# A Strassen-type feed-forward layer: forming the combined input blocks in feature-major layout from copies of transposed blocks

## The chip, the cores and the metric

The kernel runs on one core of one Trainium2 chip. The metric is the device time of one execution in microseconds (us). Before the change three runs took 2793.43, 2794.3 and 2796.57 us; the median is 2794.3 us.

The core has five engines that run side by side, each through its own queue, in order: PE (matrix products, and transposes as products with an identity matrix), DVE (the vector engine), ACT (the scalar engine), POOL (GpSimd) and SP (which issues DMAs here). PE writes only to PSUM, a small memory of eight banks, each of 512 float32 values in each of 128 partitions. SBUF is the large working memory.

## The reference

Two pre-norm layers work on a sequence of 1024 tokens of width 1024. Each has a mixer (attention), a feed-forward part (`conv_ffn`) and an embedding gate. What the change touches lies between the mixer and the feed-forward part:

```
x = x + y                                       # y: the mixer's output
x = x + conv_ffn(rms_norm(x, ffn_norm[i]), w_ffn_up[i], ...)

def conv_ffn(h, w_up, conv_w, conv_b, w_down):
    u = h @ w_up                                # 1024 -> 2 x 2816
    up = pad(u, one token on either side)
    u = up[:, :-2] * conv_w[0] + up[:, 1:-1] * conv_w[1] + up[:, 2:] * conv_w[2] + conv_b
    gate, val = split(u, 2)
    return (silu(gate) * val) @ w_down
```

## The kernel before

**Precision.** Every large product is float32 in three passes: each operand is split into a high part (a copy to the format fp32r, by ACT) and a low part (the operand less its high part, by DVE), and PE adds high x high, high x low and low x high (`mm3`, L172 to L177).

**The up-projection.** `ffn` (L309) multiplies the normed input h with `w_up` by a scheme of seven products in place of eight (Strassen's, in Winograd's form). h is cut into four quarters, by halves of the features and of the tokens. Besides the quarters themselves it needs four combinations of them, numbered 1 to 4; combination 1 overwrites a quarter that lies in `self.H`, the others go to `self.T`. For the weights the same kind of sums is made on POOL (`sums`, L395), and each weight operand is split by ACT and DVE (`prepare`, L413, with `parts`, L321). The first column of 128 features (`plain`, L335) is computed without the scheme, with the four quarters, and gives time to form the combinations. From f = 1 on each column takes six or seven products of 12 matmuls (`product`, L430), in the order `UP1` for the first and `UP` for the others.

**From the mixer to h.** The mixer ends in `gemm_part` (L242), the output projection, whose second half of the columns is walked in eight blocks of 128 tokens. For each block t, when its residual add on DVE is done (L258), `fold_mixed` (L1522) runs: the block's sum of squares on ACT (L222) and its reciprocal root on POOL (L182, L183), the scaling of block t-1 on DVE (L226), and `ready` for block t-2. `ready` (L1506) calls `to_hT` (L229). This transposes the block on PE, four 128x128 tiles into one PSUM bank, twice (L236); ACT copies the bank to the high part (L238), DVE subtracts for the low part (L239). Blocks 6 and 7 follow as `rest` during `plain`'s first half: block 6 after three steps of the gate column, block 7 after three of the value column.

**The combinations.** `ready` also keeps the scaled block, token-major (one token to a partition). With block q of the last four, `mixes(q)` (L265) forms the four combinations of blocks q-4 and q in that layout: three differences on POOL (L271, L272, L274) and one on DVE (L273), each 128x512. Later, `turn_mix` (L277) brings one combination of one block pair to feature-major layout: four transposes on PE into a PSUM bank (L283), then for combination 1 one ACT copy and one DVE subtraction of 128x512 (L288, L289), for the others two of each of 128x256 (L296, L297). Its sixteen calls a layer stand in the program order in `plain`'s second half (combinations 2 and 3, one after every second step) and in f = 1 (combinations 1 and 4, L646 to L648).

**What sets the order.** The program's order is written by hand, and every engine takes its instructions in that order. The framework adds the semaphore waits between engines. Small PSUM tiles (`tb`) rotate through four one-bank buffers: an output projection's block uses one and `to_hT` two, a turn one, and a column's first products two. SBUF tiles of 4 KB per partition come from a pool of 37 (`u`).

**The functions between.** `conv` (L360) is the convolution of a column: one ACT pass with weight and bias (L363), two DVE passes (L364, L366), and SiLU on ACT for the gate (L369). `evict` (L449) moves and adds products between PSUM banks.

Of the kernel before, what the change touches and what calls it, by code (L numbers as in the profile page):

```python
# [11 lines left out]
F32 = mybir.dt.float32  # L12
# [13 lines left out]
P = 128  # L26
S = 1024
# [79 lines left out]
class Kern:  # L107
# [118 lines left out]
        self.nc.vector.scalar_tensor_tensor(xs, x, r, gb, op0=ALU.mult, op1=ALU.mult)  # L226
        return xs

    def to_hT(self, src, t):  # L229

        nc = self.nc
        for h in range(2):
            ps = self.tb()
            v = ps.rearrange("p (k c) -> p k c", k=4)
            for k in range(4):
                nc.tensor.transpose(v[:, k, :], src(4 * h + k), self.ident)  # L236
            oh, ol = self.hT2(slice(4 * h, 4 * h + 4), slice(t * P, (t + 1) * P))
            nc.scalar.copy(oh, v)  # L238
            nc.vector.tensor_sub(ol, v, oh.bitcast(F32))  # L239


    def gemm_part(self, W, k0, load, after):  # L242
# [34 lines left out]
    def turn_mix(self, n, j):  # L277

        nc = self.nc
        src = self.tm[j].pop(n)  # L280
        ps = self.tb()
        for k in range(4):
            nc.tensor.transpose(ps[:, k * P:(k + 1) * P], src[:, k * P:(k + 1) * P], self.ident)  # L283
        jk = slice(j * P, (j + 1) * P)
        if n == 1:
            v = ps.rearrange("p (k c) -> p k c", k=4)
            h, l = self.hT2(slice(0, 4), slice(512 + j * P, 512 + (j + 1) * P))
            nc.scalar.copy(h, v)  # L288
            nc.vector.tensor_sub(l, v, h.bitcast(F32))  # L289
            return  # L290
        if n not in self.T:
            self.T[n] = [[self.u([P, 2, 512], F32R, "T") for _ in range(2)] for _ in range(2)]
        for q in range(2):
            v = ps[:, q * 256:q * 256 + 256].rearrange("p (k c) -> p k c", k=2)
            h, l = (self.T[n][x][q][:, :, jk] for x in range(2))
            nc.scalar.copy(h, v)  # L296
            nc.vector.tensor_sub(l, v, h.bitcast(F32))  # L297
# [1179 lines left out]
    def build(self):  # L1477
        nc, a = self.nc, self.a
        srcs = []
        for u in range(6):  # L1480
            srcs += [(a["w_in"][u, q], 768) for q in range(4)]
        srcs += [(a["w_out"][h, 2 * k + q], 1024) for k in range(2) for h in range(2) for q in range(2)]
        srcs += self.ffn_srcs(a, 0)
        ends = [len(srcs)]
        srcs += [(a["w_gate"][0, h, q], 1024) for h in range(2) for q in range(4)]
        for p in range(8):
            srcs += [(a["w_inc"][q, p], 1024, 0.125 if q == 0 else None) for q in range(3)]
        srcs += [(a["w_outc"][h, 2 * k + q], 1024) for k in range(2) for h in range(2) for q in range(2)]
        srcs += self.ffn_srcs(a, 1)
        ends.append(len(srcs))  # L1490
        srcs += [(a["w_gate"][1, h, q], 1024) for h in range(2) for q in range(4)]
        W = Weights(self, srcs, ends)
        self.setup(W)

        stats, scaled = {}, {}
        self.keep, self.tm = {}, {}

        def stage1(t):
            stats[t] = self.norm_stats(t)

        def stage2(t):
            for q in sorted(stats):
                if q <= t:
                    scaled[q] = self.norm_scale(*stats.pop(q))

        def ready(t, mixed=False):  # L1506
            stage2(t)
            for q in sorted(scaled):
                if q <= t:
                    x = scaled.pop(q)  # L1510
                    self.to_hT(lambda k: x[:, k * P:(k + 1) * P], q)
                    if mixed:
                        self.keep[q] = x
                        if q >= 4:
                            self.mixes(q)

        def fold(t, mixed=False):
            stage1(t)
            stage2(t - 1)
            ready(t - 2, mixed)  # L1520

        def fold_mixed(t):  # L1522
            fold(t, True)

        def rest(mixed=False):
            stage2(NT - 1)
            ready(NT - 2, mixed)
            yield
            ready(NT - 1, mixed)
            yield  # L1530

        def rest_ple(row):
            for t in range(4, NT):
                fold(t)
                yield
            self.load_gain(row)
            yield from rest()

        seen = set()

        def ready0(t):
            for q in range(t, min(t + 3, NT)):
                if q not in seen:
                    seen.add(q)
                    stage1(q)
                    self.X[q] = None
            stage2(t + 1)
            ready(t)

        W.nraw = 0  # L1550
        stage1(0)
        stage2(0)
        W.pump(1)
        ready(0)
        W.pump(1)
        stage1(1)
        W.pump(2)
        W.nraw = 2
        seen.update((0, 1))
        def load0(t):  # L1560
            if t == 0:
                self.load_gain(a["ffn_norm"][0:1, :])
            self.load_x(t, a["x"][t * P:(t + 1) * P, :])

        def load1(t):
            if t == 0:
                self.load_gain(a["ffn_norm"][1:2, :])
            self.load_x(t, self.x_dram[t])

        self.even(W, ready0, load0, fold_mixed)  # L1570
        for i in range(2):
            nc.sync.dma_start(self.cw[:, i], a["convp"][i])
        if self.stop == "mix0":
            return self.dump()
        for i in range(2):
            self.ffn(i, W, rest(True), lambda: self.ple_pre(i), fold)
            if self.stop == f"ffn{i}":
                return self.dump()
            if i == 0:
                def after(h, t):  # L1580
                    if h:
                        fold(t)
                        nc.sync.dma_start(self.x_dram[t], self.X[t])
                self.ple(0, W, rest_ple(a["attn_norm"][1:2, :]), after)
                if self.stop == "ple0":
                    return self.dump()
                self.odd(W, rest(), load1, fold_mixed)
                if self.stop == "mix1":
                    return self.dump()
            else:  # L1590
                def finish(t):
                    stage2(t)
                    for q in sorted(scaled):
                        nc.sync.dma_start(self.out[q * P:(q + 1) * P, :], scaled.pop(q))

                def after1(h, t):
                    if h:
                        stage1(t)
                        finish(t - 1)
                self.ple(1, W, rest_ple(a["final_norm"][None, :]), after1)  # L1600
                finish(NT)
# [95 lines left out]
```

## Time and profile before

| | |
|---|---|
| median of three runs | 2794.3 us |
| the profiled execution | 2795.31 us |
| its span, first to last instruction | 2793.3 us |
| transposes of the combinations on PE (L283) | 128, 18.8 us |
| transposes of the blocks on PE (L236) | 384 in all, 51.6 us |
| differences of blocks on POOL (L271, L272, L274) | 8 each, 10.3, 12.7 and 13.5 us |
| differences of blocks on DVE (L273) | 8, 8.4 us |
| layer 0: first and last transposes of combinations | 724.7 and 764.4 us |
| layer 1: the same | 2028.8 and 2068.8 us |

How to read the lines. A line of the timeline gives the start in us, the duration in us, the engine, the line of the program, the operation, the output and its inputs by the program's names, sizes and a count; several like instructions in a row are merged, and the duration is then that of all. In square brackets is the time for which the engine was idle just before, and what ended the wait. A line of the groups gives the count, then the busy time in us and the mean of one in ns, then the idle time before them. A line of the waits gives who waited for whom, the total in us, how many times, and the longest. A line of the list of one source line's instructions gives shortest, median and longest duration in ns. A line of the stretches gives the stretch, its length, the busy time of PE, of its weight loads, of DVE, ACT and POOL with the number of instructions, the granted clock of PE, and the DMAs.

### The profile page before, as it was taken

Reading aid. Unit: us, or ns where it says so; the run is one execution under the profiler, and the core shown is the slowest. Engines: PE = TensorE matmul, PEld = TensorE weight load, DVE = VectorE, ACT = ScalarE, POOL = GpSimd, SP = SyncE. Lnnn points to the kernel's source line nnn. Section 1 sums busy time; section 2 is a strip of 40 time slices with the busy share of each in tenths; the row PEclk is TensorE's granted clock in tenths of the full one; section 3 lists DMA queues with packets and bytes.
Section 4 is the critical chain, followed back from the end, with each engine's and each line's share of the span. In section 5 each row is a group of like instructions: output and inputs, shape, how many; then the busy total and the mean of one; then the engine's idle time right before and its main releaser. Section 6 shows DMA issues by size and latency. Waiting matters only on the chain. (4 is left out here: it accounts for less than half of the span.)

```text
span 2793.3 us, 37183 instructions
## 1 busy us (share of the span) xinstructions
PE 2734.1 (98%) x13776; PEld 2265.0 (81%) x13776; DVE 1920.2 (69%) x3004; ACT 1405.2 (50%) x2727; POOL 668.1 (24%) x756
## 2 busy tenths in 40 slices
PE   8999999999999999999999999999999999999998
PEld 8988877777788888888887878877878888888887
DVE  5677878775777777677635666666677777767753
ACT  4455567563444444534523666766344444453532
POOL 2222751000544444100101001000244444400000
PEclk9999999999999999999999999999999999999999
DMA  4000001101134333833211111124023343472411
GB/s 161 1 24 24 27 9 46 46 16 33 39 144 150 133 118 148 297 110 128 87 68 71 37 59 48 38 70 161 16 89 136 130 151 136 170 275 83 147 46 61
DMA packets 101700, 260.77 MB, mean 93 GB/s; under 512 B 12048, under 2 KB 18320, under 8 KB 101520
## 3 DMA queue, kind: packets, MB, share of 16 engines
q1 hardware_dynamic: 101520, 258.40, 26.1%
q8 instruction: 109, 1.79, 0.3%
q14 instruction: 71, 0.58, 0.1%
HBM read 200.16 MB, written 58.20 MB: 92 GB/s over the span
## 5 line engine op out<-in xcount | busy, mean ns | idle before, releaser
L446 PE MATMUL b<-H,op 128*128 128x512 f32 x2016 | 482.5, 391 | 9.9 <-DVE T L297 6.9
L446 PEld LDWEIGHTS b<-H,op 128*128 128x128 f32 x2016 | 379.2, 189 | 90.1 <-issue 7.5
L446 PE MATMUL S<-T,op 128*128 128x512 f32 x1512 | 364.1, 390 | 2.9 <-ACT m L464 2.7
L175 PE MATMUL b<-hi,H 128*128 128x512 f32 (+1 forms) x896 | 337.9, 377 | 1.5 <-ACT H L1297 1.5
L446 PEld LDWEIGHTS S<-T,op 128*128 128x128 f32 x1512 | 283.2, 188 | 63.3 <-ACT m L464 3.2
L176 PE MATMUL b<-lo,H 128*128 128x512 f32 (+1 forms) x896 | 329.8, 368 | 0.8 <-DVE lo L165 0.8
L177 PE MATMUL b<-hi,H 128*128 128x512 f32 (+1 forms) x896 | 330.2, 368 | 0.3 <-DVE H L1298 0.3
L182 POOL TENSOR_SCALAR col<-col 128x1 f32<-128x1 f32 (+2 forms) x100 | 29.4, 294 | 1253.3 <-ACT xs L222 1074.1
L582 PE MATMUL S<-do,do 128*128 128x512 f32 x924 | 276.7, 390 | 3.6 <-ACT do L323 2.2
L582 PE MATMUL b<-do,do 128*128 128x512 f32 x924 | 275.5, 389 | 0.0
L582 PEld LDWEIGHTS S<-do,do 128*128 128x128 f32 x924 | 172.5, 188 | 41.9 <-ACT do L323 3.0
L582 PEld LDWEIGHTS b<-do,do 128*128 128x128 f32 x924 | 173.4, 188 | 36.2
L986 ACT ACTIVATE P<-S,col 128x1024 f32<-128x1024 f32 x128 | 143.4, 1121 | 111.5 <-DVE col L977 109.0
L324 DVE TENSOR_TENSOR op<-sm,op 128x512 fp32r<-128x512 f32 x168 | 131.2, 781 | 87.8 <-ACT op L323 87.0
L175 PEld LDWEIGHTS b<-hi,H 128*128 128x128 f32 x896 | 169.4, 189 | 23.0 <-ACT H L1297 1.9
L177 PEld LDWEIGHTS b<-hi,H 128*128 128x128 f32 x896 | 169.1, 189 | 21.7 <-DVE H L1298 1.2
L176 PEld LDWEIGHTS b<-lo,H 128*128 128x128 f32 x896 | 169.6, 189 | 20.8 <-DVE lo L165 2.3
L324 DVE TENSOR_TENSOR op<-raw,op 128x512 fp32r<-128x512 f32 x126 | 161.1, 1298 | 3.8 <-ACT op L323 3.4
L977 DVE TENSOR_REDUCE col<-S 128x1 f32<-128x1024 f32 x128 | 153.1, 1217 | 10.8 <-PE S L974 9.9
L175 PE MATMUL b<-H,hi 128*128 128x512 f32 x384 | 157.3, 410 | 0.2 <-ACT H L238 0.2
L177 PE MATMUL b<-H,lo 128*128 128x512 f32 x384 | 150.1, 391 | 0.0
L176 PE MATMUL b<-H,hi 128*128 128x512 f32 x384 | 149.8, 390 | 0.2 <-DVE H L239 0.2
(199 smaller groups left out, 5275.2 us busy)
## 6 DMA issues: line engine op xcount, KB each, us to landing
raw<-in_w_up SPq DMA_DIRECT2D x88, 512.0 KB, 4.4
we<-in_w_down SPq DMA_DIRECT2D x44, 512.0 KB, 5.1
g_dram<-cv SPq DMA_DIRECT2D x44, 512.0 KB, 2.6
wt_dram<-we SPq DMA_DIRECT2D x88, 256.0 KB, 3.1
wd<-wt_dram SPq DMA_DIRECT2D x88, 256.0 KB, 2.9
wd<-in_w_down SPq DMA_DIRECT2D x66, 256.0 KB, 5.3
G<-g_dram SPq DMA_DIRECT2D x64, 256.0 KB, 5.4
raw<-in_w_inc SPq DMA_DIRECT2D x24, 512.0 KB, 3.8
```

Of the source, the lines that this page charges most:

```text
L175: mm(out, st[0], mv[0], start=start, stop=False)
L176: mm(out, st[0], mv[1], start=False, stop=False)
L177: mm(out, st[1], mv[0], start=False, stop=stop)
L182: self.nc.gpsimd.tensor_scalar(r, ss, inv_n, EPS, op0=ALU.mult, op1=ALU.add)
L324: nc.vector.tensor_sub(o[:, 1], src, o[:, 0].bitcast(F32))
L446: mm(out, w[:, x, k], moving(n, y, k), start=(fresh and k + x + y == 0), stop=(k == 3 and x == 1), skip_group_check=True)
L582: mm(out[t], A[:, x, t * P:(t + 1) * P], B[:, y], start=(fresh and k == 0 and x + y == 0), stop=(k == NC - 1 and x == 1), skip_group_check ...
L977: nc.vector.tensor_reduce(nm, ps, axis=AX.X, op=ALU.max, negate=True)
L986: nc.scalar.activation(p, ps, AF.Exp, bias=nm, accum_out=e["s"][:, c:c + 1])
```

## The change

`to_hT` gets a tile `keep` when the block belongs to the inputs of the feed-forward part. After the high copy and the low subtraction of each half, ACT copies the same PSUM bank a second time, in full precision, into that tile. `mixes` is as it was, but works on these feature-major copies, and not on the scaled token-major block. `turn_mix` no longer transposes: it takes the combination from SBUF, where the ACT copies and the DVE subtractions before took it from PSUM. Their number and sizes stay, as do their places in the program order.

```diff
-    def to_hT(self, src, t):
+    def to_hT(self, src, t, keep=None):
...
             nc.scalar.copy(oh, v)
             nc.vector.tensor_sub(ol, v, oh.bitcast(F32))
+            if keep is not None:
+                nc.scalar.copy(keep[:, h * 512:h * 512 + 512], ps)
...
         src = self.tm[j].pop(n)
-        ps = self.tb()
-        for k in range(4):
-            nc.tensor.transpose(ps[:, k * P:(k + 1) * P], src[:, k * P:(k + 1) * P], self.ident)
         jk = slice(j * P, (j + 1) * P)
         if n == 1:
-            v = ps.rearrange("p (k c) -> p k c", k=4)
+            v = src.rearrange("p (k c) -> p k c", k=4)
...
         for q in range(2):
-            v = ps[:, q * 256:q * 256 + 256].rearrange("p (k c) -> p k c", k=2)
+            v = src[:, q * 256:q * 256 + 256].rearrange("p (k c) -> p k c", k=2)
...
                     x = scaled.pop(q)
-                    self.to_hT(lambda k: x[:, k * P:(k + 1) * P], q)
                     if mixed:
-                        self.keep[q] = x
-                        if q >= 4:
-                            self.mixes(q)
+                        self.keep[q] = self.u([P, S], F32, "keep")
+                    self.to_hT(lambda k: x[:, k * P:(k + 1) * P], q, self.keep.get(q))
+                    if mixed and q >= 4:
+                        self.mixes(q)
```

## The prediction

> **What bounds the kernel now.** I read the page first, then the whole-span waits of the matrix engine, then the timeline of every engine from the last mixer product to the second feed-forward column, in both layers.
>
> ```profile
> span 2793.3 us, 37183 instructions
> PE 2734.1 (98%) x13776; PEld 2265.0 (81%) x13776; DVE 1920.2 (69%) x3004; ACT 1405.2 (50%) x2727; POOL 668.1 (24%) x756
> PE b L446 <- DVE T L297: 6.9, 2, 3.4
> PE b L446 <- DVE op L324: 3.0, 2, 1.5
> L283 PE MATMUL b<-ident,tm 128*128 128x128 f32 x128 | 18.8, 275 | 0.0
> ```
>
> PE is busy 98% of the span, so work taken off PE shortens the kernel where PE is really the last to be ready. The transposes that go are the 128 of L283. But two of PE's few waits, once per layer each, are for VectorE (DVE) in this very stretch, so there the vector side sets the pace. The profiled run took 2795.31 us, 2.0 more than its span; the median of the three runs is 2794.3, so I add differences to 2794.3. What a measurement of this kernel can tell from no change is about 0.2%, 5.6 us. Layer 1 repeats layer 0 some 1304.1 us later (the first column product: 741.49 and 2045.62), so I work layer 0 and double it.
>
> **What PE saves.**
>
> ```profile
> 728.32 0.60 PE L283 MATMUL b<-ident,tm 128*128 128x128 f32 x4
> 730.15 0.60 PE L283 MATMUL b<-ident,tm 128*128 128x128 f32 x4
> ...
> 741.49 4.34 PE L446 MATMUL b<-H,op 128*128 128x512 f32 x12 [3.43 <-DVE T L297]
> 745.63 1.31 PE L283 MATMUL b<-ident,tm 128*128 128x128 f32 x8
> ...
> 770.52 5.60 PE L446 MATMUL b<-H,op 128*128 128x512 f32 x24
> 775.96 2.88 PE L446 MATMUL S<-T,op 128*128 128x512 f32 x12
> ...
> 780.80 2.57 PE L446 MATMUL b<-H,op 128*128 128x512 f32 x10 [1.51 <-DVE op L324]
> ```
>
> 24 products take 775.96 - 770.52 = 5.44, 0.227 each. Two turns with six products between stand 1.83 apart: a turn of four transposes costs 1.83 - 6 x 0.227 = 0.47. Sixteen turns a layer are 7.5 us. The 3.43 stall before the first column product goes too: it waited for a PSUM bank that a turn held, and turns hold none afterwards. That product then took 745.63 - 741.49 = 4.14 in place of 12 x 0.227 = 2.72, another 1.42. If PE alone decided, the change would give 7.5 + 3.43 + 1.42 = 12.4 a layer, 24.7 in all: 2769.6 us. The last row says that it doesn't: 40 us on, PE still waits 1.51 for DVE. Whatever PE saves ahead of 780.80 is spent waiting there, unless DVE comes earlier. So I follow DVE.
>
> **What the copies add, in the mixer's last products.** One block of this stage before the change:
>
> ```profile
> 701.83 1.04 PE L236 MATMUL b<-ident,xs 128*128 128x128 f32 x8
> 702.80 1.06 ACT L222 ACTIVATE xs<-x 128x1024 f32<-128x1024 f32 x1 [1.53 <-issue]
> 703.86 1.06 ACT L238 CAST H<-b 128x512 fp32r<-128x512 f32 x2
> 704.46 1.29 DVE L239 TENSOR_TENSOR H<-b,H 128x512 fp32r<-128x512 f32 x2 [0.55 <-ACT H L238]
> 705.45 1.04 PE L236 MATMUL b<-ident,xs 128*128 128x128 f32 x8
> 705.67 0.68 DVE L258 TENSOR_TENSOR x<-b,x 128x512 f32<-128x512 f32 x1
> 706.38 1.06 ACT L222 ACTIVATE xs<-x 128x1024 f32<-128x1024 f32 x1 [1.46 <-DVE x L258]
> ```
>
> PE's block is 705.45 - 701.83 = 3.62. The loop square, high copies, low subtractions, residual add, next square takes 706.38 - 702.80 = 3.58. It fits with 0.04 to spare. The price of a full-precision copy out of PSUM and what a second reader of a bank has to wait for:
>
> ```profile
> L462 ACT COPY m<-b 128x512 f32<-128x512 f32 x42 | 24.6, 587 | 0.0
> ...
> 725.37 0.37 ACT L296 CAST T<-b 128x256 fp32r<-128x256 f32 x1 [4.63 <-PE b L283]
> 726.23 0.38 ACT L296 CAST T<-b 128x256 fp32r<-128x256 f32 x1 [0.49 <-DVE T L297]
> ...
> 725.77 0.42 DVE L297 TENSOR_TENSOR T<-b,T 128x256 fp32r<-128x256 f32 x1 [2.49 <-ACT T L296]
> ```
>
> The second L296 copies other columns than the first L297 reads, into another tile; all they share is the bank, and it starts only 0.04 after that subtraction ends. So the new copy waits for the subtraction ahead of it, and on ACT's queue the second half's high copy stands behind it, with its subtraction, the residual add on DVE and the next square behind that. The loop becomes: square to high copy 1.06; to its subtraction 0.60; subtraction 0.69 + 0.04 = 0.73; full copy 0.48 (two back to back take 1.06, one 0.59); second high copy 0.60; subtraction 0.61; add to square 0.71. Sum 4.79, against PE's 3.62: 1.17 too long.
>
> ```profile
> 692.59 1.06 ACT L238 CAST H<-b 128x512 fp32r<-128x512 f32 x2
> 695.38 0.48 PE L175 MATMUL b<-hi,H 128*128 128x512 f32 x1
> 707.44 1.05 ACT L238 CAST H<-b 128x512 fp32r<-128x512 f32 x2
> 712.64 1.06 PE L236 MATMUL b<-ident,xs 128*128 128x128 f32 x8 [0.48 <-DVE xs L226]
> ```
>
> PE feels it through its four banks, three of them used a block. From a high copy to the end of the second full copy is 0.60 + 0.73 + 0.48 + 0.60 + 0.73 + 0.59 = 3.73, so the first block's last bank comes free at 692.59 + 3.73 = 696.3, where the product at 695.38 needs it: 0.9 late, then 1.17 more for each of three products. The high copy of block 4 comes at 692.59 + 4 x 4.79 = 711.75 in place of 707.44. From block 4 on DVE's difference of L273 also waits for the second full copy (715.5), and the last residual add stands behind it: add 716.1, scaling 716.7 to 718.3, and the transposes at 712.64 move to about 718.5: 5.9 late. The next 24 products hide nothing of that.
>
> **What the new subtractions cost DVE.** In the turns both inputs of a low subtraction now lie in SBUF; before, one came from PSUM.
>
> ```profile
> L324 DVE TENSOR_TENSOR op<-raw,op x126: 675/1755/1790, 732.6 to 2449.1; 128x512 fp32r<-128x512 f32 x126
> L324 DVE TENSOR_TENSOR do<-wd,do x154: 682/687/699, 1144.3 to 2665.3; 128x512 fp32r<-128x512 f32 x154
> ...
> 721.48 1.81 DVE L273 TENSOR_TENSOR tm<-xs 128x512 f32<-128x512 f32 x1
> 734.62 1.27 DVE L364 SCALAR_TENSOR_TENSOR cv<-S,cw,cv 128x1023 f32<-128x1023 f32 x1
> ...
> 721.45 1.29 POOL L272 TENSOR_TENSOR tm<-xs,tm 128x512 f32<-128x512 f32 x1
> 728.39 1.28 POOL L405 TENSOR_TENSOR sm<-raw 128x512 f32<-128x512 f32 x1
> 732.24 1.30 POOL L411 TENSOR_TENSOR sm<-raw,sm 128x512 f32<-128x512 f32 x1
> ```
>
> The same subtraction takes 0.69 in the down-projection and mostly 1.76 beside POOL's sums; the L273 at 721.48 took 1.81, having started 0.03 after a POOL operation that kept its 1.29. I read from these that such an operation all but stands still until POOL's current one ends: 1.1 a time. The Trainium skill, "SBUF — State Buffer", section "Who interferes with whom", speaks against the change here: a VectorE instruction with two SBUF inputs and a GpSimd one that reads SBUF exclude each other, and the later one is blocked until the first is done. No run here shows it for a 256-wide subtraction; by the rule each of those waits as a 512-wide one does, without it they stay at 0.42, which is the second rival below.
>
> Blocks 5, 6 and 7 go through the serial order one after another: block 5's high copy at about 717.9 and its last full copy done at 721.6; block 6 held by the scaling of block 7 until 724.9 and done at 728.0; block 7 done at 731.7. There POOL still has its two last differences and the four sums of L405 to L411 to do, about six operations, which before were over at 733.5. DVE has L273 and eight 256-wide subtractions: at 0.36 apart 735.2 if nothing holds them; with six waits of 1.2 (back to back each meets nearly a whole 1.29), 742.4. Two L324 follow, 1.2 to 1.5, so L364, at 734.62 before, starts at about 743.9: 9.3 late.
>
> **What DVE gets back.** From L364 to the end of the subtraction that PE waits for at 780.80 (780.75) DVE needs 46.1 us before. It sat idle in that stretch for transposes and banks:
>
> ```profile
> 740.92 0.76 DVE L297 TENSOR_TENSOR T<-b,T 128x256 fp32r<-128x256 f32 x2 [0.56 <-ACT T L296]
> 742.11 0.76 DVE L297 TENSOR_TENSOR T<-b,T 128x256 fp32r<-128x256 f32 x2 [0.44 <-ACT T L296]
> ...
> 745.02 0.69 DVE L324 TENSOR_TENSOR op<-sm,op 128x512 fp32r<-128x512 f32 x1
> 747.16 1.29 DVE L289 TENSOR_TENSOR H<-b,H 128x512 fp32r<-128x512 f32 x2 [1.44 <-ACT H L288]
> 750.80 1.29 DVE L289 TENSOR_TENSOR H<-b,H 128x512 fp32r<-128x512 f32 x2 [1.76 <-ACT H L288]
> ```
>
> 0.56 once, 0.44 seven times, 1.44 and 1.76 are 6.8 us, and all go: ACT's copies no longer wait for a bank. Against that the eight subtractions of the fourth combination meet POOL's eight operations of that stretch. Each can hold DVE once more for 1.1 at most, and four or five of them hold an L324 already: 0 to 5.6 us, of which I take half, 2.8. DVE gets back 6.8 - 2.8 = 4.0.
>
> **The sum.** 9.3 - 4.0 = 5.3 us later a layer at the product that waits, 10.6 in both: 2794.3 + 10.6 = 2804.9. PE's own 12.4 a layer all lies ahead of that wait and is worth nothing. ACT's 32 extra copies (two halves of eight blocks in two layers, each 0.59) cost 19 us of an engine that is half idle; only their place counts. POOL's work doesn't change, only its start. The new tiles come from the pool of 37; no row here shows a wait for a free one, I take 0, and one block, 3.6, a layer is the worst I allow.
>
> **The rivals.** First, a cold matrix engine on top. The third column product needs the operand of the L324 at 745.02, done 11.1 after L364; less the 1.9 of waits gone on that way it comes at 743.9 + 9.2 = 753.1. The first product can start when its own L324 is done, at 743.2, and two products are over at 748.6: PE stands still for some 4 us, longer than in the stall that goes.
>
> ```profile
> 741.40:745.60 4.20, 4.11 (x12) 3.19 (x13) 2.79 (x7) 2.19 (x6) 0.00 (x0) 0.66 0.00 0
> ```
>
> After the 3.43 stall the granted clock was 0.66, and the product cost 1.42 more. If such a loss falls in the last products before DVE's operand, it adds 1.4 a layer: 2807.7. It decides from idle times of about 3.4 on. The Trainium skill, "TensorE: Matmul & The Clock Gate", section "What's actually happening", gives an idle window of about 3.4 us before the clock is halved; by it both the removed and the new wait lie at the edge. Second, on the other side: POOL doesn't hold the narrow subtractions, because it stands idle between its own waits or yields. Then L364 starts at 735.2 + 1.3, 1.9 late, and DVE gets back the whole 6.8: 4.9 earlier a layer, 2784.5 us, faster. It decides if fewer than about two of the six waits occur. For it speaks the shortest of the L324 on raw weights, 675 ns; against it their median, 1755. Third, the full copy runs beside the subtraction: then a block's loop is only 0.48 longer, 0.44 over PE's 3.62, and four blocks less the bank's slack lag about 1.5. POOL ends at 735.0, two L324 later L364 starts at 737.6, 3.0 late, and with 4.0 back 1 us a layer is won: 2792.3, no change that can be told. The 0.49 wait of L296 speaks against it.
>
> **How the numbers follow.** The forecast has 0.55, its own range 2800 to 2810 from the 0 to 5.6 of the fourth combination and three to six waits at the second. The cold engine has 0.13, unheld subtractions 0.17, the copy beside the subtraction 0.10, a wait for tiles 0.05 (up to 2812). Of the forecast 0.06 falls below 2799.9. Slower: 0.49 + 0.13 + 0.05 = 0.67; same: 0.10 + 0.06 = 0.16; faster 0.17. The range 2786 to 2811 leaves out about half of the second rival and the tail above, under 2 in 10.
>
> **What would show it.** Right: no L283; a full copy on ACT that starts about 0.04 after a L239 ends; blocks of about 4.8 in the last mixer products; 25.9 from the first high copy of the stage to the transposes of block 6 (20.05 before); six or more of the 256-wide subtractions of 1.2 to 1.6 before the first convolution; PE waiting for operands in the first and second columns. Wrong: blocks that stay at 3.6, or subtractions that stay at 0.42, with the first columns earlier than before.

## The result and the profile after

Six runs of the changed kernel have a median of 2803.78 us (2802.1 to 2805.64), six of the kernel before on the same chip 2793.95 us. The ratio is 1.0034, with a 95% interval of 1.0024 to 1.0045: the kernel is slower by 9.8 us. The forecast was 2804.9. The profiled execution took 2805.64 us, its span 2803.5, 10.2 more than the span before.

The head of the page of the changed kernel, and then its waits of PE over the whole span (who waited for whom, total, times, longest):

```profile
span 2803.5 us, 36914 instructions
...
PE 2730.0 (97%) x13648; PEld 2257.7 (81%) x13648; DVE 1939.2 (69%) x3004; ACT 1419.2 (51%) x2759; POOL 670.7 (24%) x756
```

```profile
PE b L445 <- ACT S L459: 12.8, 2, 6.4
PE b L175 <- ACT keep L241: 7.0, 8, 0.9
```

The 128 transposes are gone (13776 - 13648), and PE's busy time fell by only 4.1 us, where they had cost 18.8: PE got slower elsewhere. Its granted clock, the share of full speed at which PE is clocked, fell from 0.995 to 0.991 as a mean over the span. Both waits above are new. The eight for `keep` are the banks of the mixer's last products, held by the full copies. The two of 6.4 us are one a layer, before the second column product. Lines after the edit are one to three off: the turns' low subtraction, L297 before, is now L296; the first convolution's DVE pass, L364, is L363; the products, L446, are L445.

The mixer's last products in the changed kernel, from the timeline (start, duration, engine, line, operation, idle before and what ended it):

```profile
693.13 0.57 ACT L238 CAST H<-b 128x512 fp32r<-128x512 f32 x1
...
701.69 1.06 ACT L222 ACTIVATE xs<-x 128x1024 f32<-128x1024 f32 x1
701.73 0.50 PE L175 MATMUL b<-hi,H 128*128 128x512 f32 x1 [0.89 <-ACT keep L241]
...
703.35 0.69 DVE L239 TENSOR_TENSOR H<-b,H 128x512 fp32r<-128x512 f32 x1 [0.50 <-ACT H L238]
...
704.07 0.59 ACT L241 COPY keep<-b 128x512 f32<-128x512 f32 x1 [0.76 <-DVE H L239]
704.55 0.59 ACT L238 CAST H<-b 128x512 fp32r<-128x512 f32 x1
...
706.50 1.06 ACT L222 ACTIVATE xs<-x 128x1024 f32<-128x1024 f32 x1
...
719.20 1.07 PE L236 MATMUL b<-ident,xs 128*128 128x128 f32 x8 [1.89 <-ACT H L238]
...
727.18 1.03 PE L236 MATMUL b<-ident,xs 128*128 128x128 f32 x8
```

Square to square is 706.50 - 701.69 = 4.81. The subtraction ends at 704.04, the full copy starts at 704.07, and the second half's high copy stands behind it. PE stops once a block, for 0.9.

The eight low subtractions of combination 2, the first convolution and what follows, on DVE; then the products that PE makes of it:

```profile
733.24 9.36 DVE L296 TENSOR_TENSOR T<-tm,T 128x256 fp32r<-128x256 f32 x8
...
743.72 1.27 DVE L363 SCALAR_TENSOR_TENSOR cv<-S,cw,cv 128x1023 f32<-128x1023 f32 x1
...
749.07 2.77 DVE L296 TENSOR_TENSOR T<-tm,T 128x256 fp32r<-128x256 f32 x8 [2.75 <-ACT T L295]
...
761.63 2.14 DVE L296 TENSOR_TENSOR T<-tm,T 128x256 fp32r<-128x256 f32 x2 [1.22 <-ACT T L295]
...
767.64 2.93 DVE L296 TENSOR_TENSOR T<-tm,T 128x256 fp32r<-128x256 f32 x2
```

```profile
752.23 5.49 PE L445 MATMUL b<-H,op 128*128 128x512 f32 x12 [6.41 <-ACT S L459]
757.52 3.16 PE L445 MATMUL S<-T,op 128*128 128x512 f32 x12
...
785.53 2.56 PE L445 MATMUL b<-H,op 128*128 128x512 f32 x10 [0.38 <-DVE op L323]
...
796.85 3.34 PE L445 MATMUL b<-H,op 128*128 128x512 f32 x14
```

Eight like subtractions take 9.36 us at 733.24 and 2.77 at 749.07: at the first POOL is at work, at the second it is idle. The product that waited 1.51 at 780.80 now starts at 785.53, 4.7 later. The one of the next column that starts here at 796.85 stood in the kernel before at:

```profile
791.46 5.60 PE L446 MATMUL b<-H,op 128*128 128x512 f32 x24
```

So at this point layer 0 is 5.4 us late. Of that, 0.54 was there at the stage's first high copy already (693.13 against 692.59), and in the fourth column the lag reaches 6.05 (816.55 against 810.50) and stays there in the columns behind. The stage thus costs 5.5 us in layer 0. In layer 1 it costs 5.5 again: the lag goes from 4.63 (at 1950.05 before) to 10.13 (at 2130.10); between the two it makes up 1.4. The spans differ by 10.2.

### The profile page after: what moved, and what is told of

It reads as the page before. It is cut to its first block, busy times and chain, and to the rows that moved or that the text cites. A ratio compares the mean times of both kernels' runs of the same rounds, so it can differ in the third digit from the quotient of the medians.

```text
span 2803.5 us, 36914 instructions
## 1 busy us (share of the span) xinstructions
PE 2730.0 (97%) x13648; PEld 2257.7 (81%) x13648; DVE 1939.2 (69%) x3004; ACT 1419.2 (51%) x2759; POOL 670.7 (24%) x756
## 5 line engine op out<-in xcount | busy, mean ns | idle before, releaser
L445 PE MATMUL b<-H,op 128*128 128x512 f32 x2016 | 483.3, 392 | 13.8 <-ACT S L459 12.8
L445 PEld LDWEIGHTS b<-H,op 128*128 128x128 f32 x2016 | 381.5, 189 | 95.4 <-ACT S L459 13.7
L445 PE MATMUL S<-T,op 128*128 128x512 f32 x1512 | 366.4, 391 | 5.1 <-DVE S L469 4.4
L445 PEld LDWEIGHTS S<-T,op 128*128 128x128 f32 x1512 | 284.6, 189 | 67.6 <-issue 6.5
L323 DVE TENSOR_TENSOR op<-sm,op 128x512 fp32r<-128x512 f32 x168 | 126.5, 753 | 83.9 <-ACT op L322 83.9
L323 DVE TENSOR_TENSOR op<-raw,op 128x512 fp32r<-128x512 f32 x126 | 169.4, 1364 | 2.1 <-ACT op L322 2.1
```

The source lines that it names most:

```text
L323: nc.vector.tensor_sub(o[:, 1], src, o[:, 0].bitcast(F32))
L445: mm(out, w[:, x, k], moving(n, y, k), start=(fresh and k + x + y == 0), stop=(k == 3 and x == 1), skip_group_check=True)
```

## The experiments

The theory was that of the prediction. A: PE's saving is worth nothing, because DVE is last; the loss comes from the full copies' place in ACT's queue and from POOL, which holds subtractions that now read SBUF twice. The rivals: the copies' work or memory as such, a slower matrix engine after the new 6.4 us stall, or nothing at all but PE. Medians below stand against runs of the kernel before on the same chip: 2794.45 us beside the first four experiments, 2794.56 beside the next four, 2794.9 beside the last two.

**1. The full copies behind both subtractions.** The changed kernel, with ACT's order high, high, full, full.

```diff
             nc.scalar.copy(oh, v)
             nc.vector.tensor_sub(ol, v, oh.bitcast(F32))
-            if keep is not None:
-                nc.scalar.copy(keep[:, h * 512:h * 512 + 512], ps)
+            banks.append(ps)
+        if keep is not None:
+            for h, ps in enumerate(banks):
+                nc.scalar.copy(keep[:, h * 512:h * 512 + 512], ps)
```

> The change, but the two full-precision copies of a block come after both low subtractions (ACT: high, high, full, full), so no high copy and no low subtraction stands behind a full copy. Theory A (the full copy waits for the subtraction on its PSUM bank and holds the next half's high copy, so a block's loop of 4.8 us replaces one of 3.6): blocks of 3.6 to 3.7 again in the mixer's last products, the transposes of block 6 some 5 us earlier than with the change, the first convolution's L363 at 737 to 739 in place of 743.7, and 5 to 6.5 us a layer off: 2791 to 2794 us, about the time before. Rival B (what costs is only the 256-wide subtractions beside POOL; the lag of the blocks is hidden by the 48 products of the first half column): 2801 to 2804. Rival C (it is the number of extra copies, not their place): no change, 2803.

Measured: 2792.66 us, ratio to the kernel before 0.9994 (0.9985 to 1.0004). Its timeline:

```profile
701.62 1.06 ACT L222 ACTIVATE xs<-x 128x1024 f32<-128x1024 f32 x1 [0.22 <-DVE x L263]
...
702.68 1.05 ACT L239 CAST H<-b 128x512 fp32r<-128x512 f32 x2
704.01 1.19 ACT L244 COPY keep<-b 128x512 f32<-128x512 f32 x2 [0.27 <-DVE H L240]
705.24 1.06 ACT L222 ACTIVATE xs<-x 128x1024 f32<-128x1024 f32 x1
...
712.51 1.06 PE L237 MATMUL b<-ident,xs 128*128 128x128 f32 x8 [1.27 <-ACT H L239]
...
723.35 11.56 DVE L299 TENSOR_TENSOR T<-tm,T 128x256 fp32r<-128x256 f32 x8
...
736.04 1.27 DVE L366 SCALAR_TENSOR_TENSOR cv<-S,cw,cv 128x1023 f32<-128x1023 f32 x1
...
744.55 4.59 PE L448 MATMUL b<-H,op 128*128 128x512 f32 x12 [6.38 <-ACT S L462]
```

Nothing was taken away: the same 32 copies run, in the gap in which ACT would wait for DVE anyway. Square to square is 3.62 again (705.24 - 701.62), the transposes of block 6 stand at 712.51, where they were before (712.64). So 11 us of loss hung on the order of two instructions. All transposes of the combinations are gone in this kernel, and still it can't be told from the kernel before: PE's 12.4 us a layer bought nothing that can be told. PE reaches its first column product at 734.05, 7.4 earlier than before, and then stands still for 6.38 us, for ACT. What this stall costs by itself the run does not tell. All eight subtractions of combination 2 are held here, 11.56 in all, and yet the first convolution, at 736.04, comes ahead of the expected 737 to 739.

**2. The copies alone.** The kernel before, with its transposes, and the full copies added at the changed kernel's place; nobody reads them.

```diff
             nc.vector.tensor_sub(ol, v, oh.bitcast(F32))
+            if keep is not None:
+                nc.scalar.copy(keep[:, h * 512:h * 512 + 512], ps)
```

> The kernel before, with its transposes of the combinations, plus the 32 full-precision copies in the change's place, into tiles that nobody reads. Theory A: blocks of 4.8 us, block 6's transposes 5 to 6 us late, the first convolution about 5 us late, and nearly all of it kept at the product that waits for DVE: 2802 to 2806 us. Rival B (only the subtractions beside POOL cost): 2794 to 2796.

Measured: 2806.67 us, ratio 1.0044 (1.0029 to 1.0059), 12.2 us slower and a little above the expected 2802 to 2806. Its timeline of PE:

```profile
701.28 0.50 PE L175 MATMUL b<-hi,H 128*128 128x512 f32 x1 [0.92 <-ACT extra L241]
...
718.47 1.07 PE L236 MATMUL b<-ident,xs 128*128 128x128 f32 x8 [1.63 <-ACT H L238]
```

The waits and the delay of block 6 (718.47 against 712.64) are those of the changed kernel, with none of the rest of the change. Experiment 1 has as many copies without harm, so it is their place that costs the 12.2. For the rest of the change experiment 1 gives -1.8, which can't be told from nothing. Together 10.4, close to the measured 9.8.

**3. POOL's sums without reading.** The changed kernel, with POOL's four weight sums of the column f = 1 replaced by writes of a constant of the same size: the column's sums are left out of the computation.

```diff
             o = sm[f, which]
-            if which == 1:
+            if f == 1:
+                pool.memset(o, 1.0)
+            elif which == 1:
```

> The change, but POOL's four weight sums of the column f = 1 in each layer are memsets of the same tiles, which read nothing (the sums of that column are left out, its operands are constants). Theory A with the second cause (a DVE subtraction with two SBUF inputs stands still while a POOL operation reads SBUF): of the eight 256-wide subtractions in the first column only those beside the two remaining differences wait, 9.4 us for the eight become 4 to 5.5, L363 of the first convolution comes 4 to 5 us earlier, and 3.5 to 5 us a layer are won: 2794 to 2797 us. Rival C2 (the eight subtractions are slow by themselves, or wait for something else than POOL's reads): 9.4 us stay, 2802 to 2804.

Measured: 2796.76 us, ratio 1.0009 (0.9999 to 1.0018), 7.0 less than the changed kernel. DVE:

```profile
732.40 4.96 DVE L296 TENSOR_TENSOR T<-tm,T 128x256 fp32r<-128x256 f32 x8
...
738.50 1.27 DVE L363 SCALAR_TENSOR_TENSOR cv<-S,cw,cv 128x1023 f32<-128x1023 f32 x1
```

The subtractions are the same, and 9.36 became 4.96. But the four writes are also shorter than the sums: 1.92 us together, where the sums took 5.8. So the time alone does not tell whether reading or length held DVE. The subtractions beside the writes do. POOL's writes, and the six subtractions from 735.28 on:

```profile
735.02 1.92 POOL L404 MEMSET sm<- 128x512 f32 x4
```

```profile
L296 DVE TENSOR_TENSOR T<-tm,T x6: 411/412/414, 735.3 to 737.0; 128x256 fp32r<-128x256 f32 x6
```

Each took 0.41, as one that nothing holds. The first two of the eight stand beside POOL's last differences, which read, and took 1.5 each. The 4.4 us appear as 3.5 a layer in the time, so DVE is on the path there.

**4. PE kept busy.** The changed kernel, with 20 spare matrix products into an unused bank after the first column product, in the place of the new stall.

```diff
                 product(f, s)
                 if (f, s) == (1, 0):
+                    spare = self.tb()
+                    for _ in range(20):
+                        mm(spare, self.H[0, 0, 0][:, 0, :P], self.H[0, 0, 0][:, 0], start=True, stop=True)
                     evict(1, 0)
```

> The change, plus 20 products per layer into a spare bank right behind the first column product, 4.5 us of the 6.4 in which PE stands still there, so that its clock should not fall. If the cold clock is part of the loss (the second column product took 5.3 us in place of 2.7): that product back at 2.7 to 3.0, and up to 2.5 us a layer off, 2798.5 to 2801 us. If DVE alone sets the end of this stretch: the product is fast again but the time stays, 2802 to 2804.

Measured: 2803.65 us, ratio 1.0034 (1.0022 to 1.0047): as the changed kernel. PE, and then the stretch of that product in the same run (length, busy times, the granted clock as the third figure from the end):

```profile
751.70 4.55 PE L445 MATMUL b<-H,op 128*128 128x512 f32 x12 [1.86 <-ACT S L459]
```

```profile
751.70:756.05 4.35, 4.35 (x13) 3.40 (x14) 3.94 (x7) 4.35 (x8) 0.00 (x0) 0.63 0.00 0
```

The stall shrank from 6.41 to 1.86 us, and the product from 5.29 to 4.35; the time didn't move. The clock fell even after 1.86 us of waiting, so the experiment did not keep PE at full speed there. It doesn't test the stall either: the spare products only fill it, and the second column product starts nearly where it did (751.70 against 752.23). The 0.94 us won on that product were lost again: PE then waited 2.07 for DVE's add before 772.00, where the changed kernel waited 1.47, and the product behind it was slow in its turn (4.38 for eleven matmuls in place of 2.81). What the run does show is that the clock as a whole is not the loss. Over the span its six runs were granted 0.993 to 0.996, as the kernel before beside them, and the changed kernel 0.991 to 0.994; the time is the same.

The next ones look for a version that beats both kernels, and so test where DVE's time goes once the copies are in place. All start from experiment 1.

**5. All differences on DVE.** POOL keeps only the sums.

```diff
-        sub = self.nc.gpsimd.tensor_sub
+        sub = self.nc.vector.tensor_sub
```

> The changed kernel with the copies behind both subtractions (the order of the first experiment, 2792.66 us), and all four differences of a block pair on DVE, where three stood on POOL. Theory A: with the copies in place, what still eats PE's 12.4 us a layer is DVE beside POOL. DVE takes 12 differences of 128x512 more, 0.69 each, 8.3 us a layer; but they fall in the last mixer blocks, where DVE has gaps of 0.5 to 0.65 after each ACT copy, and the eight subtractions of combination 2, which take 11.56 us in the first experiment, should fall to between 3 and 6, since POOL's four sums, freed of twelve differences, run before them. Net 3 to 4 us a layer earlier: 2784 to 2788 us. Theory B, DVE is short of time and not of peace: 8.3 us more work a layer delays the first convolution by 2 us or more: 2793 to 2800 us. Theory C, the stall before the second column product (6.4 us, ACT's queue) decides by itself: no change, 2791 to 2794 us.

Measured: 2786.5 us, ratio 0.9971 (0.9959 to 0.9983). DVE:

```profile
728.42 2.77 DVE L299 TENSOR_TENSOR T<-tm,T 128x256 fp32r<-128x256 f32 x8
...
732.31 1.28 DVE L366 SCALAR_TENSOR_TENSOR cv<-S,cw,cv 128x1023 f32<-128x1023 f32 x1
```

Theory A, and clearer than expected: DVE got twelve instructions a layer more and reached its convolution at 732.31 in place of 736.04, because eight subtractions fell from 11.56 to 2.77. POOL's four sums ran from 713.64 to 721.75, ahead of them. DVE was not short of time, it was held.

**6. Combination 3 split.** Differences on POOL as in experiment 1. The ACT copies of the combination's four turns stand in the gate half, ahead of the SiLU; their eight low subtractions behind the first convolution.

```diff
-                        if h == 1 and k % 2 == 1:
+                        if h == 1 and gv == 0 and k % 2 == 1:
                             self.turn_mix(*turns.pop(0))
+                            self.turn_mix(*turns.pop(0), later)
...
                         conv(0, 0, ps[0])
+                        for x in later:
+                            nc.vector.tensor_sub(*x)
```

> The order of the first experiment (2792.66 us), and the turns of combination 3 split: their ACT copies stand in the gate half, ahead of the first SiLU, and their eight low subtractions on DVE behind the first convolution's two passes. Differences stay on POOL. In the first experiment DVE is idle for 2.75 us behind that convolution, since the ACT copies of these turns stand behind the SiLU and its table load. Theory A (DVE's time decides): the 2.75 are filled and the copy of the column's bank leaves ACT about 2.4 us earlier, so the stall before the second product falls from 6.4 to about 4 us, and the end comes 2 to 2.7 us a layer earlier: 2787 to 2789 us. Theory C (the stall decides): also earlier, by the 2.4 of the stall, 2788 us; the two differ in the fifth run's outcome. Theory D: the chain to the fourth column's adds runs through the subtractions of combination 4 beside POOL's sums, which start when the products do, so nothing is won: 2791 to 2794 us.

Measured: 2788.99 us, ratio 0.9978 (0.9969 to 0.9987), at the end of the expected range. PE:

```profile
741.96 4.34 PE L454 MATMUL b<-H,op 128*128 128x512 f32 x12 [3.97 <-ACT S L468]
...
763.34 3.03 PE L454 MATMUL S<-T,op 128*128 128x512 f32 x12 [2.65 <-DVE S L478]
```

The stall fell to 3.97, as worked out. The wait of 2.65, for an add of the first column ahead of the product that stands second in the second column's order, stayed: in this kernel too DVE is late there. Whether DVE's filled gap or PE's shorter stall brought the 3.7 us, this run does not tell apart; both theories gave the same.

**7. Both edits.**

> Both edits together: differences on DVE and the turns of combination 3 split. Theory A: the gains add, since one ends before the convolution and the other after it: 5 to 6.5 us a layer, 2780 to 2783 us. Rival: once the first is there PE is last, and the second wins nothing more: within 2 us of the kernel with the differences on DVE.

Measured: 2786.58 us, ratio 0.9973 (0.9962 to 0.9984): the rival held, the second edit adds nothing. PE:

```profile
728.83 0.50 PE L176 MATMUL S<-H,hi 128*128 128x512 f32 x1 [2.24 <-DVE H L240]
```

But not because PE had become last in general: there is a new wait of 2.24 in the value half, for block 7's low subtraction, which stands on DVE behind the four differences of block 6, and the one for the add stayed, 2.66 before 764.18.

**8. Combination 4 late.** As 7, with its four turns all behind the sixth product of the first column.

```diff
-                for _ in range(2 if s < 2 else 1):
+                for _ in range({0: 2, 1: 2, 5: 4}.get(s, 0)):
```

> As the one before, and the four turns of combination 4, which stand after the third to the sixth product of the first column, all moved behind its sixth product. There they met POOL's sums for the second column, two 256-wide subtractions taking 2.9 us in place of 0.75, ahead of the add that PE waits for (2.66 us in the first experiment). Theory A: that wait goes, 2 to 3 us a layer earlier than the kernel without it, if the four turns are still done when the second column's second product needs them: 2775 to 2779 us. Rival: the turns then delay the add and the convolution of the first column's gate half by the 3 us they take, and the second product waits for them: no better, or 2 to 4 us later.

Measured: 2782.95 us, ratio 0.9957 (0.9944 to 0.9969); 3.6 better than 7, where 4 to 6 were expected, and above the expected 2775 to 2779. PE, then a stretch of it:

```profile
726.08 0.50 PE L176 MATMUL S<-H,hi 128*128 128x512 f32 x1 [2.22 <-DVE H L240]
...
738.50 2.88 PE L454 MATMUL b<-H,op 128*128 128x512 f32 x12
...
762.00 2.83 PE L454 MATMUL S<-T,op 128*128 128x512 f32 x11 [1.65 <-DVE T L300]
```

```profile
726.08:730.60 4.52, 4.52 (x13) 3.56 (x14) 4.36 (x9) 4.51 (x14) 0.00 (x0) 0.65 0.09 12
```

The wait of 2.66 for the add is gone; the second column's second product now waits 1.65 for the turns, so the rival had a part of it.

**9. Block 6's differences behind block 7.** As 8, with the four differences of block 6 after block 7's low subtractions.

```diff
-                    if mixed and q >= 4:
-                        self.mixes(q)
+                    if mixed and q >= 4 and q != 6:
+                        for z in (6, 7) if q == 7 else (q,):
+                            self.mixes(z)
```

> The fastest version so far (copies behind both subtractions, differences on DVE, the turns of combination 3 split, those of combination 4 late: 2782.95 us), with the differences of block 6 moved behind the subtractions of block 7. In it PE still waits 2.22 us a layer for block 7's low subtraction, which stands on DVE behind the four differences of block 6, and these meet POOL's sums. Theory A (PE is now last there): the wait goes and the product that ended late comes up to 2.2 us a layer earlier, 2779 to 2781 us. Rival (DVE still decides in the first two columns, where PE waits 1.0, 1.65 and 0.86 us for it): the wait is found again there, 2782 to 2784 us.

Measured: 2777.99 us, ratio 0.9939 (0.9926 to 0.9953), the fastest of all, 16.9 us below the kernel before and 1 below the expected 2779 to 2781. PE, then a stretch of it:

```profile
734.51 2.88 PE L454 MATMUL b<-H,op 128*128 128x512 f32 x12
```

```profile
726.00:730.60 4.60, 4.60 (x22) 3.82 (x21) 4.50 (x11) 3.87 (x9) 0.00 (x0) 1.00 0.22 62
```

The first column product comes 4.0 us earlier than in 8, and only 2.2 of it is the wait. Most of the rest is the clock: 0.65 granted over 4.52 us in 8 is 0.35 x 4.52 = 1.6 us lost, and here the clock stays at 1.00. The profiled execution was the fastest of its five (2775.34 us); by the medians the gain over 8 is 5.0 us in both layers together.

**10. The kernel before, rearranged.** Its transposes kept, all differences on DVE, combination 4 late. It asks whether the edits of 5 and 8 alone bring the gain.

> The kernel before, with its transposes of the combinations, and two of the edits that helped the changed one: all four differences on DVE, and the turns of combination 4 behind the sixth product of the first column. It tells whether the gain over the kernel before comes from those edits alone. Theory A: the change itself carries it, since PE keeps the 7.5 us of transposes a layer, and DVE, which set the pace before, gets 8.3 us of differences more: 2790 to 2797 us. Rival: the edits by themselves are worth the 11 us, so this kernel takes 2781 to 2786 us too.

Measured: 2803.93 us, ratio 1.0035 (1.0023 to 1.0048): slower than the kernel before, further off than theory A had it. PE:

```profile
721.68 1.94 PE L236 MATMUL b<-ident,xs 128*128 128x128 f32 x8 [2.45 <-DVE xs L226]
...
770.07 5.46 PE L446 MATMUL b<-H,op 128*128 128x512 f32 x12 [0.60 <-DVE T L297]
```

DVE's differences delay the scaling of block 7, and its transposes stand at 721.68 where they were at 719.02; the late turns, which need banks, then hold a product. So these two edits pay only with the change. The splitting of combination 3 and the order of 9 were not tried on the kernel before.

## Why the prediction was right, point by point

**PE's saving is worth nothing: held.** Experiment 1 has every transpose removed and no harm from the copies, and its time is that of the kernel before. The step that carried this was the wait of 1.51 for DVE at 780.80, some 40 us behind the first column product. The place was another, though: in the changed kernel PE gave its time back earlier, in the 6.41 us before the second column product and in 1.47 for DVE's add before 773.02, and at that wait only 0.38 was left (785.53).

**The copies: held.** 4.79 was predicted for a block, 4.81 measured; 25.9 from the first high copy to the transposes of block 6, 719.20 - 693.13 = 26.07 measured. The third rival, a copy that runs beside the subtraction, fell with the row at 704.07. The Trainium skill, "PSUM — Partial Sum Buffer", section "PSUM bank collisions raise a hardware error", has ScalarE and VectorE reading the same partitions of one bank at the same time as an error, and asks for a semaphore by bank and quarter of the partitions, or simply by bank. The trace agrees so far as the copy at 704.07 stood idle for 0.76 and was released by DVE's subtraction of the same bank. That the two must not overlap is the page's word, and no run here tried it.

**The subtractions beside POOL: held.** Eight took 9.36, 6.6 more than the 2.77 of those that nothing held: six took 1.51 each and two 0.41. Six waits of 1.2, 7.2, were predicted. The first convolution stood at 743.72, predicted 743.9. Experiments 3 and 5 show the cause, and the second rival, which would have made the kernel faster, fell with it. The Trainium skill, "SBUF — State Buffer", section "Who interferes with whom", says that such a VectorE instruction contends with a GpSimd one that reads SBUF and not with one that only writes; experiment 3 agrees: 0.41 us each beside the writes, where the changed kernel has 1.51 beside the sums.

**What DVE gets back: held in sum, not in its parts.** 4.0 was predicted. At the prediction's own point (780.80 before, 785.53 now) the lag is 4.7 with a convolution that was 9.1 later (743.72 - 734.62), so 4.4 came back. The idle times of 6.8 all went, but one of 1.22 came, before 761.63, for ACT's casts. The subtractions of combination 4 cost more than the 2.8 taken: the four pairs took 0.75, 2.14, 2.93 and 1.22, 7.0 together, where four unheld pairs take about 2.8, so 4.2 more. Against that the ten operand subtractions of this stretch (L324, now L323) took 9.0 in place of 11.5, which the sum does not hold. Nor does it hold what comes behind that point: PE waits for two more of DVE's adds, 0.49 before 794.02 and 0.40 before 813.73, and the lag grows from 4.7 to 6.05. Less the 0.54 that was there before, a layer costs 5.5, where the sum has 5.3. That these are so close is in part luck.

**The first rival named the wrong place.** It put PE's stall of some 4 us before the third column product, for DVE's operand. It came before the second, 6.41 us, for ACT. ACT's queue in the changed kernel:

```profile
746.39 1.28 ACT L368 ACT_TABLE_LOAD   x1 [8.07 <-DVE cv L365]
747.68 1.06 ACT L368 ACTIVATE cv<-cv 128x1024 f32<-128x1024 f32 x1
748.65 2.53 ACT L295 CAST T<-tm 128x256 fp32r<-128x256 f32 x8
...
751.61 0.57 ACT L459 COPY S<-b 128x512 f32<-128x512 f32 x1
```

The second product adds to a bank that ACT must copy first, and that copy stands behind the SiLU, which waits for the late convolution, and behind eight casts. The step that failed is the one that followed only DVE's operand into these products and did not walk ACT's queue. The product then took 757.52 - 752.23 = 5.29 in place of 2.72, more than the rival's 1.42. By experiment 4 the slow product did not matter for the time. What the stall itself costs was not tested alone; its end hangs on the convolution that DVE was late with, and behind it PE waited for DVE once more (1.47 before 773.02). So the forecast's number came out right although PE's stall was larger than any in the text, and that part of it is luck.

## What to carry to other kernels

Before pricing work taken off the busiest engine, look for its last wait behind that work: if another engine is late there, the saving is spent waiting. When a PSUM bank gets a second reader, put the new read behind everything that others wait for; the order of two instructions was worth 11 us here, more than the whole change cost. And when an operand moves from PSUM to SBUF, ask who else reads SBUF just then: moving the differences from POOL to a VectorE that seemed the bottleneck made the changed kernel faster (2792.66 to 2786.5 us).

## What the runs showed of the hardware that was not expected

Pauses shorter than the 3.43 us of the prediction lowered PE's clock too, and it was not their length alone that decided. In the changed kernel PE paused 1.89 us before block 6, up to 719.20. Two stretches of 3.41 us there (PE's busy time is the second figure behind the stretch, its clock the third from the end):

```profile
717.10:720.51 3.41, 1.52 (x11) 1.29 (x11) 2.64 (x3) 2.29 (x5) 3.20 (x3) 1.00 0.00 0
720.51:723.92 3.41, 3.41 (x9) 2.65 (x9) 2.32 (x3) 1.48 (x3) 3.30 (x3) 0.50 0.00 0
```

Experiment 4 has the same pause of 1.89 at the same place, up to 718.64:

```profile
715.27:718.68 3.41, 1.52 (x8) 0.97 (x7) 3.02 (x4) 1.90 (x4) 2.92 (x2) 1.00 0.01 2
718.68:722.10 3.42, 3.42 (x20) 2.96 (x21) 1.62 (x3) 2.05 (x4) 3.17 (x5) 1.00 0.00 0
```

The first lowered the clock to 0.50 for 3.41 us, the second left it at 1.00. From that block's transposes to the next one's, at 727.18, PE took 7.98 in the changed kernel, and 6.38 in experiment 4 (718.64 to 725.02). Other pauses fall out both ways too: one of 1.51 in the kernel before (1876.36 to 1877.87) lowered the clock, one of 2.67 in experiment 5 (759.54 to 762.21) did not; the 2.22 of experiment 8 did, the 2.24 of experiment 7 at the same place did not.

The traces show one more thing. The clock was 1.00 or 0.50 (figures between are means over a stretch), and in each of the twelve traces the stretches at 0.50 start a whole number of 3.41 us apart: in the changed kernel at 720.51 and at 747.82, 8 x 3.41 later. If each trace is cut into stretches of 3.41 us on that grid, then at full clock none in which PE stood still for less than 1.4 us was followed by one at 0.50, each with more than 1.9 was, and between the two both happened. So it matters how a pause lies on the grid. The Trainium skill, "TensorE: Matmul & The Clock Gate", section "What's actually happening", has the clock halved after an idle window of about 3.4 us, one that runs freely. The grid of 3.41 agrees with that window, but the window did not have to be idle throughout: some 1.4 us of standing still could be enough. So for a pause of about 2 us one has to look and can't rely on its length. What decides between 1.4 and 1.9 us was not found.
